# The gate values of a hybrid trunk as one product of 512 columns per layer, and their normalisation in one chain

## The chip, the cores and the metric

The kernel runs on one core of one Trainium2 chip. The metric is the device time of one execution in microseconds, the median of several runs. A core has a matmul engine (TensorE, PE in the profile) with its own loading of weights (PEld), VectorE (DVE), ScalarE (ACT), GpSimd (POOL) and SyncE (SP), which here issues the loads. Each engine works through its own queue in order; semaphores tie the queues together.

## The reference

Two layers over 512 tokens of 1024 numbers, all float32. Each layer has a mixing block (a gating MLP beside differential attention) and a convolutional feed-forward block.

```python
D_SGU, SGU_GROUPS, CHUNK = 512, 4, 128      # gate values: 4 groups of 128 columns
...
n = rmsnorm(h, attn_norm[l])
proj = n @ w_in[l]
u, v_sgu, q, k, v_att = jnp.split(proj, [...], axis=-1)
v_sgu = jax.nn.gelu(v_sgu)
vg = rmsnorm(v.reshape(B, S, SGU_GROUPS, SGU_GROUP_DIM), v_gain)      # per token and group
mixed = jnp.einsum('gpq,bcqgd->bcpgd', w, vg) + b_s.T[None, None, :, :, None]   # w: lower triangle of w_s
y_sgu = u * mixed
...
q = apply_partial_rope(q, cos, sin); k = apply_partial_rope(k, cos, sin)
scores = einsum('bqhmd,bkhmd->bhmqk', qb, kb) * scale     # softmax, difference of two maps, times v
```

The change touches only how `v_sgu` (the gate values) is computed and normalised.

## The kernel before

**Arithmetic.** A float32 product is made from three fast products of numbers split into a high and a low part: high by high, high by low, low by high. A split is a cast (the high part, names that end in h) and a subtraction (the low part, names in l). Weights come in blocks of 128x1024 (`raw`), which ScalarE casts to `wh`, and GpSimd (in halves of 512) or VectorE subtracts to `wl`. Names carry the number of the block: `wh8` is block 8; layer 1's blocks begin at 96, so block 104 is to layer 1 what block 8 is to layer 0. Loads run two blocks ahead of the products (`AHEAD`).

**Input products.** The 128x512 activations `gh_a`, `gl_a` (one of 8 per contraction step k) meet the weights in stages: gate values (`vs`), q, k, attention values (`va`), u. Gate values and va have tokens on the partitions (`tok_gemm`: per k and token tile t three products of 256 columns, two token tiles in a bank); q, k and u have features there (`feat_gemm`: products of 512 columns). The gate values of two pairs of groups, gp 0 and 1, are separate stages. In layer 0 the first of them runs with q in one loop (`both_first`), from half tiles of weights that `opening()` loads and splits itself (`or`, `oh`, `ol`); nine idle products stand ahead of it on TensorE. Then in both layers: the other gate half, k of heads 0 and 1, va, and the score phase.

**What sets the order.** The code is written out in the order in which each engine gets it: `pin` (L119) ties every instruction to the one before it on its engine, so nearly all rows carry L119. `products()` is a generator of steps, one per k; after each step `run` pops one piece of work off the list `due` for the other engines. Forty steps run before the scores, then `flush()` empties `due`. In the score phase each unit (head, query tile) takes one more step and one piece off `later`.

**Work on the gate values.** `gate_work(gp, banks)` makes gelu on ScalarE (`vs`), squares (`vq`, ScalarE), sums (VectorE, `gs`), the reciprocal root of 8 columns (`rsqrt`, 12 small VectorE operations), the normalisation (`normed`, VectorE) and the split (`part`, `vg`). `spatial()` masks the weights `wsp` on GpSimd and splits them (`wsh`, `wsl`). `rope` turns q and k: per head a shuffle (`q_0sh`) and a product from the bank (`q_0t`) on VectorE, a product and a sum on GpSimd (for k's first head on VectorE), then a split (`q_0h`, `q_0l`). The scores of unit 0 read `q_0h`, `q_0l`, `k_0h`, `k_0l`.

In layer 0 the second gate half's work beyond gelu lies in `later`:

```python
g = gate_work(1, banks)
due.extend(g[:2])
later.extend([lambda: (spatial(), g[2](), g[3]())] + g[4:])
```

In layer 1 all of it, and `spatial()`, is done before the scores; `later` has only the split of k's second head.

Of the kernel before, what the change touches and what calls it, by code (L numbers as in the profile page):

```python
# [21 lines left out]
P = 128  # L22
# [47 lines left out]
def trunk(ctx: ExitStack, tc, a, out):  # L70
# [72 lines left out]
    for l in range(DEPTH):  # L143
        specs += [a["w_in"][l, c] for c in range(20)]
# [11 lines left out]
    def block(i):  # L156
        while len(loaded) <= min(i + AHEAD[0], len(specs) - 1):
            j = len(loaded)
            n = specs[j].shape[-1]
# [6 lines left out]
            (sync if j < 6 else nc.sync).dma_start(out=raw, in_=specs[j])  # L166
# [10 lines left out]
    def opening():  # L177

        first = [[], []]
        for m in range(KD):  # L180
            sync.dma_start(out=hT[m], in_=a["xT"][m])
            c = slice(m % 2 * 256, m % 2 * 256 + 256)
            if m % 2 == 0:
                tiles = [(fslot(f"or{b}_{m}"), slot(f"oh{b}_{m}"), slot(f"ol{b}_{m}")) for b in range(2)]
            for b, (r, h, lo) in enumerate(tiles):
                spec = specs[2 * b + m // 4]
                sync.dma_start(out=r[:, c], in_=spec[:, m % 4 * 256 : (m % 4 + 1) * 256])
                first[b].append((h[:, c], lo[:, c]))
# [5 lines left out]
            for b, (r, h, lo) in enumerate(tiles):  # L194
# [51 lines left out]
    def tok_step(banks, x, w, first, last):  # L246
        (xh, xl), (h, lo) = x, w
        for t in range(NT):
            ts = slice(t * P, (t + 1) * P)
            o = banks[t // 2][:, t % 2 * 256 : t % 2 * 256 + 256]  # L250
            mm(o, xh[:, ts], h, start=first and t % 2 == 0, stop=False)
            mm(o, xh[:, ts], lo, start=False, stop=False)
            mm(o, xl[:, ts], h, start=False, stop=last and t % 2 == 1)

    def tok_gemm(banks, xs):

        for k, x in enumerate(xs):
# [3 lines left out]
            tok_step(banks, x, (h[:, c], lo[:, c]), k == 0, k == len(xs) - 1)  # L261
            yield

# [188 lines left out]
    for l in range(DEPTH):  # L452
# [101 lines left out]
        vg, us, ya, ys = [None] * 2, [None] * NG, [None] * NH, [None] * NG  # L554

        def gate_work(gp, banks):

            gs = sm.tile([P, 8], F32, tag="gs", name=f"gs{l}_{gp}", bufs=2)
            vts, sqs, vg[gp] = [None] * 2, [None] * 2, [None] * 2
            r = []  # L560

            def gelu(b):
                vts[b] = tmp(f"vs{l}_{gp}_{b}")
                for x in range(2):
                    c = slice(x * 256, x * 256 + 256)
                    t = 2 * b + x
                    act.activation(vts[b][:, c], banks[b][:, c], AF.Gelu_apprx_tanh, scale=norm.rcol[:, t : t + 1])

            def square(b):
                sqs[b] = tmp(f"vq{l}_{gp}_{b}")  # L570
                act.activation(sqs[b], vts[b], AF.Square)

            def sums(b):
                dve.reduce_sum(
                    gs[:, 4 * b : 4 * b + 4], sqs[b].rearrange("p (x d) -> p x d", d=P), axis=mybir.AxisListType.X
                )
# [5 lines left out]
            def normed(b):  # L582
                v3 = vts[b].rearrange("p (x d) -> p x d", d=P)
                rb = r[0][:, 4 * b : 4 * b + 4].unsqueeze(2).to_broadcast([P, 4, P])
                dve.tensor_tensor(out=v3, in0=v3, in1=rb, op=ALU.mult)

            def part(b):
# [598 lines left out]
```

## Time and profile before

| | |
|---|---|
| median of 3 runs | 1136.31 us (1135.13 to 1136.41) |
| profiled execution | 1136.36 us, of which its span is 1134.6 us |
| TensorE busy | 1115.3 us, 98% of the span |
| VectorE, ScalarE, GpSimd busy | 687.8, 478.4, 412.6 us |
| mean granted clock of TensorE | .996 of full |

The span runs from the first to the last instruction that the trace holds; 1.76 us of the execution lie around it. Busy times are sums over the whole span, so a stage can have another limit than the mean. Matmuls overlap in the records: the pitch from start to start is their cost, not the listed length.

### The profile page before, as it was taken

The numbers are of one execution on the slowest core, as the hardware profiler recorded it, in microseconds if no ns is written. First come the engines' busy times: TensorE is split into PE (matmuls) and PEld (weight loads), VectorE is DVE, ScalarE is ACT, GpSimd is POOL, SyncE is SP. The second block draws the span as 40 slices with busy tenths as digits, with TensorE's granted clock in tenths as the row PEclk, the third lists the DMA queues.
The fourth block names the chain that finished last, engine by engine and source line by source line (L and its number), as shares of the span: only waits on it lengthen the run. The fifth ranks groups of instructions, "written<-read, shape, count | busy, mean of one in ns | idle before, by whom it ended". The sixth has DMA issues, their size and how long they took to land.

```text
span 1134.6 us, 14944 instructions
## 1 busy us (share of the span) xinstructions
PE 1115.3 (98%) x5637; PEld 935.4 (82%) x5637; DVE 687.8 (61%) x1271; ACT 478.4 (42%) x810; POOL 412.6 (36%) x390
## 2 busy tenths in 40 slices
PE   9998999999999999999999999999999999999996
PEld 7986888888888888888899788888888888888886
DVE  7778874775662247664357887767657522666634
ACT  6453553544442134443334554454444312444351
POOL 0466333533222103333557642353313310332351
PEclk9999999999999999999999999999999999999998
DMA  8221112332333232223332221122233323222322
GB/s 272 75 82 50 57 65 94 95 104 89 104 93 97 91 110 93 93 84 93 103 120 80 77 73 57 56 92 95 95 109 93 96 92 110 93 93 93 92 76 75
DMA packets 34215, 105.24 MB, mean 93 GB/s; under 512 B 4064, under 2 KB 8544, under 8 KB 34144
## 3 DMA queue, kind: packets, MB, share of 16 engines
q1 hardware_dynamic: 33712, 104.27, 28.7%
q8 instruction: 44, 0.72, 0.3%
q14 instruction: 27, 0.22, 0.1%
q10 hardware_dynamic: 432, 0.03, 0.0%
HBM read 102.19 MB, written 2.10 MB: 92 GB/s over the span
## 4 chain that ended last, share of the span: by engine, by line
PE 85%; DVE 9%; ACT 3%; POOL 2%; issue 1%; DVEq 0%; ACTq 0%; POOLq 0%
PE g L119 21%; PE v L119 21%; PE dn L119 19%; PE wo L119 7%; PE u L119 4%; PE vs L119 3%; PE q L119 3%; PE dl L119 3%; PE sc L119 1%; ACT wh L119 1%; DVE s L119 1%; PE mx L119 1%; PE av L119 1%; POOL wl L119 1%; ACT s L119 1%
## 5 line engine op out<-in xcount | busy, mean ns | idle before, releaser
L119 POOL TENSOR_TENSOR wl<-raw,wh 128x512 fp32r<-128x512 f32 x187 | 255.4, 1387 | 567.2 <-ACT wh L119 556.4
L119 ACT CAST wh<-raw 128x1024 fp32r<-128x1024 f32 (+1 forms) x192 | 194.3, 1015 | 373.2 <-issue 180.3
L119 DVE TENSOR_TENSOR wl<-raw,wh 128x1024 fp32r<-128x1024 f32 (+1 forms) x96 | 121.2, 1263 | 131.7 <-ACT wh L119 131.6
L119 PE MATMUL v<-gh_f,wh 128*128 128x512 f32 x352 | 137.3, 390 | 0.0
L119 PE MATMUL v<-gh_f,wl 128*128 128x512 f32 x352 | 137.0, 389 | 0.0
L119 PE MATMUL v<-gl_f,wh 128*128 128x512 f32 x352 | 137.0, 389 | 0.0
L119 PE MATMUL g<-gh_f,wl 128*128 128x512 f32 x352 | 137.0, 389 | 0.0
L119 PE MATMUL g<-gh_f,wh 128*128 128x512 f32 x352 | 136.9, 389 | 0.0
L119 PE MATMUL g<-gl_f,wh 128*128 128x512 f32 x352 | 136.9, 389 | 0.0
L119 DVE SCALAR_TENSOR_TENSOR cv<-up_cv,par,cv 128x512 f32<-128x512 f32 x88 | 74.0, 885 | 6.4 <-ACT cv L119 6.1
L119 PEld LDWEIGHTS v<-gh_f,wl 128*128 128x128 f32 x352 | 66.1, 188 | 13.8
L119 PEld LDWEIGHTS g<-gl_f,wh 128*128 128x128 f32 x352 | 66.1, 188 | 13.7
L119 PEld LDWEIGHTS g<-gh_f,wl 128*128 128x128 f32 x352 | 66.1, 188 | 13.7
L119 PEld LDWEIGHTS g<-gh_f,wh 128*128 128x128 f32 x352 | 66.1, 188 | 13.7
L119 PEld LDWEIGHTS v<-gl_f,wh 128*128 128x128 f32 x352 | 66.1, 188 | 13.6
L119 PEld LDWEIGHTS v<-gh_f,wh 128*128 128x128 f32 x352 | 66.1, 188 | 13.6
L119 DVE SCALAR_TENSOR_TENSOR cg<-up_cg,par,cg 128x512 f32<-128x512 f32 x88 | 69.6, 841 | 6.0 <-ACT cg L119 5.6
L119 DVE TENSOR_TENSOR up_cv<-v,rstd_f 128x512 f32<-128x512 f32 x44 | 30.2, 692 | 67.3 <-PE v L119 67.2
L119 DVE TENSOR_TENSOR up_cg<-g,rstd_f 128x512 f32<-128x512 f32 x44 | 30.0, 691 | 57.8 <-PE g L119 54.9
L119 ACT ACTIVATE s<-s,mn 128x128 f32<-128x128 f32 (+3 forms) x64 | 35.5, 555 | 60.1 <-DVE mn L119 55.3
L119 DVE TENSOR_TENSOR hT<-dn,hT 128x512 f32<-128x512 f32 x28 | 19.1, 690 | 46.7 <-PE dn L119 46.7
L119 ACT ACTIVATE cg<-cg 128x512 f32<-128x512 f32 x44 | 27.7, 630 | 45.8 <-DVE cg L119 45.8
(604 smaller groups left out, 2611.2 us busy)
## 6 DMA issues: line engine op xcount, KB each, us to landing
raw<-in_w_up SPq DMA_DIRECT2D x88, 512.0 KB, 3.4
raw<-in_w_dn SPq DMA_DIRECT2D x40, 512.0 KB, 3.5
raw<-in_w_in SPq DMA_DIRECT2D x36, 512.0 KB, 3.4
raw<-in_w_out SPq DMA_DIRECT2D x16, 512.0 KB, 3.4
hT<-in_xT SPq DMA_DIRECT2D x8, 256.0 KB, 4.5
or<-in_w_in SPq DMA_DIRECT2D x16, 128.0 KB, 4.2
raw<-in_w_dn SPq DMA_DIRECT2D x8, 256.0 KB, 3.4
out<-y SPq DMA_DIRECT2D x8, 256.0 KB, 2.2
```

The costliest lines, as they stand in the source:

```text
L119: return lambda *args, **kw: pin(getattr(self.engine, op)(*args, **kw))
```

## The change

The weights of the gate values become four wide blocks per layer (two contraction steps by 512 columns, each filled by two transfers), first in the layer's list. `tok_wide` makes per step and token tile three products of 512 columns, each token tile in a bank of its own: banks 0 and 1 are of the kind that scores use, 2 and 3 of the products' kind. Both layers now run gate values, q, k, va in this order. `opening()` loads tiles of 512 columns by two transfers and splits each in one cast and one subtraction. `gate_work` works by token tile, with one sum tile of 16 columns and one root. Of the normalisation and split, token tiles 0 and 1 come before the scores, 2 and 3 in units 1 to 4 of the score phase. `spatial()` stands at the same step in both layers.

```diff
@@ block
-            (sync if j < 6 else nc.sync).dma_start(out=raw, in_=specs[j])
+            queue = sync if j < 6 else nc.sync
+            if wide:
+                for at, half in enumerate(specs[j]):
+                    o = raw.rearrange("p (k i c) -> p i k c", k=2, i=2)[:, at]
+                    queue.dma_start(out=o, in_=half.rearrange("p (k c) -> p k c", k=2))
+            else:
+                queue.dma_start(out=raw, in_=specs[j])
@@ opening
+            r, h, lo = fslot(f"or{m}"), slot(f"oh{m}"), slot(f"ol{m}")
+            for i, half in enumerate(specs[m // 2]):
+                sync.dma_start(out=r[:, i * 256 : i * 256 + 256], in_=half[:, m % 2 * 256 : m % 2 * 256 + 256])
+            first.append((h, lo))
             if m == 0:
-                r, h, lo = tiles[0]
-                dve.tensor_copy(h[:, c], r[:, c])
-                dve.tensor_sub(lo[:, c], r[:, c], h.bitcast(F32)[:, c])
+                dve.tensor_copy(h, r)
+                dve.tensor_sub(lo, r, h.bitcast(F32))
             norm.scaled(m)
-            for b, (r, h, lo) in enumerate(tiles):
-                if m > 0 or b > 0:
-                    act.copy(h[:, c], r[:, c])
-                    dve.tensor_sub(lo[:, c], r[:, c], h.bitcast(F32)[:, c])
+            if m > 0:
+                act.copy(h, r)
+                dve.tensor_sub(lo, r, h.bitcast(F32))
@@ tok_wide (new)
+    def tok_wide(banks, xs, ws=None):
+        for k, x in enumerate(xs):
...
+            for t in (0, 2):
+                tok_step([(t + i, banks[t + i], True, True) for i in range(2)], x, w, k == 0, k == len(xs) - 1)
+                yield
@@ gate_work
+            gs = sm.tile([P, NT * NG], F32, tag="gs", name=f"gs{l}", bufs=1)
...
-                r.append(rsqrt(gs, 8, f"gr{l}_{gp}"))
+                r.append(rsqrt(gs, NT * NG, f"gr{l}"))
@@ products
-            if l == 0:
-                yield from both_first()
-                banks = value_banks(1, sc_bank)
-                yield from tok_gemm(banks, xs)
-                g = gate_work(1, banks)
-                due.extend(g[:2])
-                later.extend([lambda: (spatial(), g[2](), g[3]())] + g[4:])
-            else:
-                yield from gate_values(0)
-                yield from queries(0)
-                yield from gate_values(1)
+            banks = [sc_bank(f"vs{t}_{l}") for t in range(2)] + [mm_bank(f"vs{t}_{l}") for t in (2, 3)]
+            yield from tok_wide(banks, xs, first if l == 0 else None)
+            gelu, sums, root, normed, part = gate_work(banks)
...
+            due.extend(([nothing] * 4 if l == 0 else []) + [of(gelu, 2, 3), of(gelu, 0, 1)])
+            q = query_banks(0)
+            yield from feat_gemm(q, xs)
+            turn0, turn1, part0, part1 = rope(q, qs, 0, "q")
+            due.extend([turn0, turn1, of(sums, 0, 1), of(sums, 2, 3), root, part0, part1])
+            due.extend(of(f, t) for f in (normed, part) for t in range(2))
+
+            later.extend(of(f, t) for f in (normed, part) for t in (2, 3))
@@ steps of a layer
         run(steps, 28 - (22 if l == 0 else 15))
-        if l > 0:
-            spatial()
+        spatial()
         run(steps, 12)
```

The queue of GpSimd in layer 0, from block 7's low part on, before (the last number of a name is a tile's own):

```order
L119 TENSOR_TENSOR wl7_571<-raw7_569,wh7_570 128x512 x2
L119 TENSOR_TENSOR q0_0sh_634<-q0_0sh_634,sr0_619 128x512
L119 TENSOR_TENSOR q0_0t1_636<-q0_0t1_636,q0_0sh_634 128x512
L119 TENSOR_TENSOR q0_1sh_652<-q0_1sh_652,sr0_619 128x512
L119 TENSOR_TENSOR q0_1t1_654<-q0_1t1_654,q0_1sh_652 128x512
L119 TENSOR_TENSOR wl8_663<-raw8_661,wh8_662 128x512 x2
L119 TENSOR_TENSOR wl9_718<-raw9_716,wh9_717 128x512 x2
L119 TENSOR_TENSOR wl10_761<-raw10_759,wh10_760 128x512 x2
```

and after:

```order
L119 TENSOR_TENSOR wl7_483<-raw7_481,wh7_482 128x512 x2
L119 TENSOR_TENSOR wl8_540<-raw8_538,wh8_539 128x512 x2
L119 TENSOR_TENSOR q0_0sh_551<-q0_0sh_551,sr0_521 128x512
L119 TENSOR_TENSOR q0_0t1_553<-q0_0t1_553,q0_0sh_551 128x512
L119 TENSOR_TENSOR q0_1sh_563<-q0_1sh_563,sr0_521 128x512
L119 TENSOR_TENSOR q0_1t1_565<-q0_1t1_565,q0_1sh_563 128x512
L119 AFFINE_SELECT wsp0_281<-wsp0_281 128x512
L119 TENSOR_TENSOR wsl0_284<-wsp0_281,wsh0_283 128x512
L119 TENSOR_TENSOR wl9_598<-raw9_596,wh9_597 128x512 x2
```

Block 8's low part moved ahead of q's rope, and the spatial weights (`wsp`, `wsl`), which stood far behind, moved between the rope and block 9.

The queue of VectorE in layer 0, around the first root, before; the first piece ends with the root's first operation, the second begins with its last:

```order
L119 STREAM_SHUFFLE q0_1sh_652<-q1_0_308 128x512
L119 TENSOR_TENSOR q0_1t1_654<-q1_0_308,cr0_611 128x512
L119 TENSOR_REDUCE gs0_0_505<-vq0_0_0_674 128x4
L119 TENSOR_REDUCE gs0_0_505<-vq0_0_1_682 128x4
L119 TENSOR_TENSOR q0_0l_713<-q0_0t1_636,q0_0h_712 128x512
L579 TENSOR_SCALAR gs0_0_505<-gs0_0_505 128x8
```

and, still before, the second piece:

```order
L389 SCALAR_TENSOR_TENSOR gr0_0_693<-gr0_0t_694,gr0_0_693 128x8
L119 TENSOR_TENSOR q0_1l_730<-q0_1t1_654,q0_1h_729 128x512
L119 TENSOR_TENSOR vs0_0_0_588<-vs0_0_0_588,gr0_0_693 128x512
L119 TENSOR_TENSOR vs0_0_1_603<-vs0_0_1_603,gr0_0_693 128x512
L119 TENSOR_TENSOR vg0_0_0l_754<-vs0_0_0_588,vg0_0_0h_753 128x512
L119 TENSOR_TENSOR vg0_0_1l_779<-vs0_0_1_603,vg0_0_1h_778 128x512
L119 STREAM_SHUFFLE k0_0sh_824<-k0_0_659 128x512
```

and the same two places after:

```order
L119 STREAM_SHUFFLE q0_1sh_563<-q1_0_443 128x512
L119 TENSOR_TENSOR q0_1t1_565<-q1_0_443,cr0_513 128x512
L119 TENSOR_REDUCE gs0_441<-vq0_0_575 128x4
L119 TENSOR_REDUCE gs0_441<-vq0_1_578 128x4
L119 TENSOR_REDUCE gs0_441<-vq0_2_587 128x4
L119 TENSOR_REDUCE gs0_441<-vq0_3_590 128x4
L594 TENSOR_SCALAR gs0_441<-gs0_441 128x16
```

and its second piece:

```order
L409 SCALAR_TENSOR_TENSOR gr0_610<-gr0t_611,gr0_610 128x16
L119 TENSOR_TENSOR q0_0l_630<-q0_0t1_553,q0_0h_629 128x512
L119 TENSOR_TENSOR q0_1l_640<-q0_1t1_565,q0_1h_639 128x512
L119 TENSOR_TENSOR vs0_0_504<-vs0_0_504,gr0_610 128x512
L119 TENSOR_TENSOR vs0_1_506<-vs0_1_506,gr0_610 128x512
L119 TENSOR_TENSOR vg0_0l_685<-vs0_0_504,vg0_0h_684 128x512
L119 TENSOR_TENSOR vg0_1l_701<-vs0_1_506,vg0_1h_700 128x512
L119 STREAM_SHUFFLE k0_0sh_716<-k0_0_536 128x512
```

There are four sums instead of two ahead of the root, and the root's columns are 16 instead of 8. The low part of q's first head moved from ahead of the root to behind it; from there to k's shuffle the rest stands as before.

## Rows read from the trace of the kernel before

**Rows 1.** Part 1 of the page: busy us, share of span, instructions

```profile
PE 1115.3 (98%) x5637; PEld 935.4 (82%) x5637; DVE 687.8 (61%) x1271; ACT 478.4 (42%) x810; POOL 412.6 (36%) x390
```

**Rows 2.** Timeline of TensorE, layer 1: start, length, instruction, wait before it

```profile
566.11 0.28 PE L119 MATMUL vs<-wh,gh_a 128*128 128x256 f32 x1
...
577.62 0.40 PE L119 MATMUL q<-gh_a,wh 128*128 128x512 f32 x1
...
601.01 0.40 PE L119 MATMUL k<-gh_a,wh 128*128 128x512 f32 x1
...
611.92 0.28 PE L119 MATMUL va<-wh,gh_a 128*128 128x256 f32 x1
...
624.13 0.33 PE L119 MATMUL sc<-k_0l,q_0h 64*128 64x128 f32 x2 [0.29 <-DVE k_0l L119]
...
624.50 0.50 PE L119 MATMUL q<-gh_a,wh 128*128 128x512 f32 x1
```

**Rows 3.** Timeline of TensorE, layer 0, and the first wo of layer 1

```profile
41.88 0.40 PE L119 MATMUL k<-gh_a,wh 128*128 128x512 f32 x1
...
64.87 0.50 PE L119 MATMUL q<-gh_a,wh 128*128 128x512 f32 x1
...
157.88 0.45 PE L119 MATMUL wo<-yah,wh 128*128 128x512 f32 x1
...
713.37 0.44 PE L119 MATMUL wo<-yah,wh 128*128 128x512 f32 x1
```

**Rows 4.** Timeline of TensorE, the opening of layer 0

```profile
1.28 4.02 PE L119 MATMUL idle<-zeros 128*128 128x512 bf16 x9 [1.28 <-DVE zeros L136]
...
4.74 0.77 PE L119 MATMUL vs<-oh,gh_a 128*128 128x256 f32 x1
...
6.83 0.37 PE L119 MATMUL vs<-ol,gh_a 128*128 128x256 f32 x1
7.04 0.28 PE L119 MATMUL vs<-oh,gl_a 128*128 128x256 f32 x1
...
8.90 0.28 PE L119 MATMUL vs<-oh,gh_a 128*128 128x256 f32 x1
```

**Rows 5.** Timeline of ScalarE, the opening: the second half tile

```profile
5.62 0.40 ACT L119 CAST oh<-or 128x256 fp32r<-128x256 f32 x1 [0.98 <-DMA or<-in_w_in]
```

**Rows 6.** Timeline of VectorE, layer 0: the first root (L384 to L389 by rsqrt)

```profile
46.65 1.25 DVE L579 TENSOR_SCALAR gs<-gs 128x8 f32<-128x8 f32 x1
...
51.69 0.17 DVE L388 TENSOR_TENSOR gr_0t<-gr_0t,gr 128x8 f32<-128x8 f32 x1
```

**Rows 7.** Timeline of GpSimd, layer 0, around the same root

```profile
40.88 1.29 POOL L119 TENSOR_TENSOR q_0sh<-q_0sh,sr 128x512 f32<-128x512 f32 x1 [2.14 <-DVE q_0sh L119]
...
46.13 5.49 POOL L119 TENSOR_TENSOR wl<-raw,wh 128x512 fp32r<-128x512 f32 x4
```

**Rows 8.** Timeline of VectorE, layer 1, gate sums to k_0l

```profile
607.33 1.28 DVE L119 TENSOR_REDUCE gs<-vq 128x4 f32<-128x512 f32 x2 [1.82 <-ACT vq L119]
...
614.94 1.29 DVE L119 TENSOR_TENSOR vs<-vs,gr 128x512 f32<-128x512 f32 x2
...
617.54 0.75 DVE L119 STREAM_SHUFFLE k_0sh<-k 128x512 f32<-128x512 f32 x1
...
622.62 1.45 DVE L119 TENSOR_TENSOR k_0l<-k_0t,k_0h 128x512 fp32r<-128x512 f32 x1
```

**Rows 9.** Timeline of GpSimd, layer 1, the spatial weights

```profile
609.13 0.63 POOL L119 TENSOR_SCALAR_AFFINE_SELECT wsp<-wsp 128x512 f32<-128x512 f32 x1
...
610.49 1.30 POOL L119 TENSOR_TENSOR wsl<-wsp,wsh 128x512 fp32r<-128x512 f32 x1 [0.73 <-ACT wsh L119]
```

**Rows 10.** Timeline of ScalarE, layer 1, the cast of a block of weights

```profile
604.27 1.05 ACT L119 CAST wh<-raw 128x1024 fp32r<-128x1024 f32 x1
```

**Rows 11.** Windows at the end: start:end, length, busy us by engine, granted clock, DMA

```profile
1124.00:1126.00 2.00, 0.41 (x2) 0.20 (x2) 1.34 (x4) 0.51 (x1) 0.00 (x0) 1.00 0.95 332
1126.00:1128.00 2.00, 0.40 (x2) 0.40 (x3) 1.31 (x7) 0.20 (x1) 0.00 (x0) 0.65 0.00 0
```

More of the change, by code (lines that the diff above doesn't have):

```diff
@@ L143, in trunk @@
     for l in range(DEPTH):
-        specs += [a["w_in"][l, c] for c in range(20)]
+        w = a["w_in"][l]
+        specs += [[w[c + k // 4][:, k % 4 * 256 : k % 4 * 256 + 512] for c in (0, 4)] for k in range(0, KD, 2)]
+        specs += [w[c] for c in [2, 3] + list(range(6, 20))]
         specs += [a["w_out"][l, c] for c in range(8)]
@@ L158, in block @@
             j = len(loaded)
-            n = specs[j].shape[-1]
+            wide = isinstance(specs[j], list)
+            n = 1024 if wide else specs[j].shape[-1]
             if j >= len(specs) - 6:
@@ L244, in feat_gemm, with tok_step @@
             yield
-    def tok_step(banks, x, w, first, last):
+    def tok_step(outs, x, w, first, last):
         (xh, xl), (h, lo) = x, w
-        for t in range(NT):
+        for t, o, opens, closes in outs:
             ts = slice(t * P, (t + 1) * P)
-            o = banks[t // 2][:, t % 2 * 256 : t % 2 * 256 + 256]
-            mm(o, xh[:, ts], h, start=first and t % 2 == 0, stop=False)
+            mm(o, xh[:, ts], h, start=first and opens, stop=False)
             mm(o, xh[:, ts], lo, start=False, stop=False)
-            mm(o, xl[:, ts], h, start=False, stop=last and t % 2 == 1)
+            mm(o, xl[:, ts], h, start=False, stop=last and closes)
     def tok_gemm(banks, xs):
+        outs = [(t, banks[t // 2][:, t % 2 * 256 : t % 2 * 256 + 256], t % 2 == 0, t % 2 == 1) for t in range(NT)]
         for k, x in enumerate(xs):
@@ L552, in values, with gate_work, gelu, sums @@
             ])
[L554 to L559, printed above, removed]
+        vg, us, ya, ys = [None] * NT, [None] * NG, [None] * NH, [None] * NG
+        def gate_work(banks):
+            gs = sm.tile([P, NT * NG], F32, tag="gs", name=f"gs{l}", bufs=1)
+            vts, sqs = [None] * NT, [None] * NT
             r = []
[L562 to L573, printed above, removed]
+            def gelu(t):
+                vts[t] = tmp(f"vs{l}_{t}")
+                act.activation(vts[t], banks[t], AF.Gelu_apprx_tanh, scale=norm.rcol[:, t : t + 1])
+            def sums(t):
+                sqs[t] = tmp(f"vq{l}_{t}")
+                act.activation(sqs[t], vts[t], AF.Square)
                 dve.reduce_sum(
-                    gs[:, 4 * b : 4 * b + 4], sqs[b].rearrange("p (x d) -> p x d", d=P), axis=mybir.AxisListType.X
+                    gs[:, NG * t : NG * t + NG], sqs[t].rearrange("p (g d) -> p g d", d=P), axis=mybir.AxisListType.X
                 )
@@ L622, in mix @@
                 osl = bm[:, t * P : (t + 1) * P]
-                vh, vl = vg[g // 2][t // 2]
-                o = (t % 2 * 2 + g % 2) * P
-                vsl = slice(o, o + P)
+                vh, vl = vg[t]
+                vsl = slice(g * P, g * P + P)
                 mm(osl, vh[:, vsl], ws_h[:, g, :], start=True, stop=False)
```

54 lines of the change are left out of this document (17 added, 37 removed).

## The prediction

> **What bounds the kernel now.** I read the page's busy times first: TensorE works 1115.3 of the span's 1134.6 us [rows 1], so an edit can gain by shortening TensorE's own work and loses wherever TensorE has to wait. Next, TensorE's timeline of layer 1's input products [rows 2]: gate values 0 take 566.11 to 577.62, k starts at 601.01, va at 611.92. In these stretches nothing waits. A gate half is 96 products of 256 columns in 11.51 us, .1199 each; k is 48 products of 512 columns in 10.91 us, .2273 each. The first break comes at the scores: the second score product starts at 624.13 after waiting .29 for k_0l, and the scores end at 624.50. So k's chain on VectorE and GpSimd already ends last here, by a little. In layer 0 the scores end at 64.87, 22.99 after k's start at 41.88 [rows 3]. The score phases, from the end of these scores to the first wo, do the same products in both layers, yet take 93.01 us in layer 0 (64.87 to 157.88) and 88.87 in layer 1 (624.50 to 713.37) [rows 2, 3].
>
> **TensorE's own work.** The change replaces 192 products of 256 columns per layer by 96 of 512: 192 x .1199 - 96 x .2273 = 23.0 - 21.8, about 1.2 us per layer, **-2.4**. The Trainium skill ("TensorE: Matmul & The Clock Gate", section on 56 against 53.3 ns) has another figure: a fixed cost of about 2.5 ns per product at the full clock. The two pitches of the rows give 2 x .1199 - .2273 = 12.5 ns per product instead. By the page the saving would be an estimated .5 us over both layers and the time 1.9 us later; the rows are this kernel's, so I keep -2.4.
>
> **The opening of layer 0.** Now the first product starts at 4.74, from a half tile of 256 columns [rows 4]; the next half lands at 5.62 [rows 5]. After the change one cast of 512 columns needs both halves. A cast of 256 took .40 on ScalarE there; I take .6 for 512 on VectorE, so the first product starts at 6.2. Its low part (a subtraction of 512 columns, .65 by half of the pair at 614.94 [rows 8]) allows the second at 6.85, and the low part of the activations, now behind it on VectorE, the third near 7.5. Nine products remain of k=0: 9 x .23 ends it near 9.7 at the full clock. Before, k=0 ended at 8.90, and the same pair of levels shows there: a product that starts at 6.83 is followed .21 later, from 7.04 on the records are as short as in layer 1. The clock rose 5.7 us after TensorE began at 1.28 with its nine idle products, without a break. Now there are breaks from 5.3 to 7.5, so the rise may come later. Both bounds: +.8 if it still rises at 7.0, and +2.2 if all nine products run at the lower level (.43 each). I take the late one, nearest to what the row shows (the rise followed unbroken work). k then starts at 41.88 - 1.2 + 2.2 = 42.9 (41.5 with the early rise).
>
> **The transfers.** The wide blocks come by two transfers each instead of one. Blocks are loaded two ahead (AHEAD), and at 566.11 and 601.01 TensorE goes over to the next product without a wait for weights [rows 2], so I take 0. Were that cover gone, the nearest such wait is the opening's .98 [rows 5].
>
> **The chain to the scores.** This decides. Call k's start S. What follows is a schedule in order of the queues, made with durations from rows.
> - ScalarE's cast of wh8 takes 1.05 [rows 10] and waits for a tile that q frees at S. GpSimd's wl8 now stands before the rope of q, not behind it; two such operations take 2.7 (5.49 for four [rows 7]): it ends at S+3.7. This is 104 in place of 8 in layer 1.
> - The rope's four operations took 40.88 to 46.13, 5.25 [rows 7]: the first head is done at S+6.3, the second at S+8.9. The selection wsp (.63) follows to S+9.5; wsl starts .73 later and takes 1.30, to S+11.6 [rows 9]. Then wl9 and wl10, 1.3 for each half.
> - ScalarE's fourth square needs the tile that q_0t's sum frees at S+6.3; with a reduction of .64 (half of 1.28 [rows 8]) the root can begin at S+7.6.
> - The root is 12 small operations on VectorE, now 12 for all four token tiles instead of twice 12. Free, one takes .17 (51.69). But at 46.65 the first one lasted 1.25, and the others lasted as long until GpSimd's wl of 46.13 ended at 51.62 [rows 6, 7]: each operation on SBUF that starts beside a GpSimd operation ends with it. So operations 1 and 2 end at S+8.9 and S+9.5 (rope and wsp), 3 to 6 fit into GpSimd's pause, 7 ends with wsl at S+11.6, 8 to 11 with the halves of wl9 and wl10 at S+16.8, the twelfth at S+17.0. Half of the operations on the chain is thus dear, as in layer 0 before.
> - Behind the root on VectorE, before k's first shuffle, stand q_0l, q_1l, two normed and two vg low parts: 6 x .65 (1.29 for two [rows 8]) = 3.9, to S+20.9.
> - From k's shuffle (617.54) to the end of k_0l (622.62 + 1.45) were 6.53 us [rows 8], and the scores ended .43 after it [rows 2]: they end at S+27.8.
>
> Without any wait it would be S+23.0, as layer 0 shows. Layer 1: S = 601.01 - 1.2 = 599.8, scores end at 627.6 instead of 624.50, **+3.1**. Layer 0: 42.9 + 27.8 = 70.7 instead of 64.87, **+5.8** (both contain the saving and the opening). The waiting of TensorE is some 4.8 us per layer, in two pieces, for k_0h and then for k_0l, with little work between.
>
> **The score phases.** Before, layer 0's units 1 to 8 carried the second gate half's squares, sums, root and the spatial weights; this leaves them. Its phase should come down to layer 1's, 93.01 - 88.87 = 4.14. What remains in both layers are two normed and two parts more in units 1 to 4 than layer 1 had; I take .3 for them (bounds 0, hidden under the products of a unit, and 2.6, four operations of .65 all exposed): **-3.8** and **+.3**.
>
> **The clock.** At the end of the kernel TensorE had .41 us of work from 1124 to 1126 at the full clock, .40 in the next two with a mean clock of .65 [rows 11]: with only the two levels that is full speed until about 1126.6 and half of it after. So it falls to 1.2 GHz some 2.6 us after work thins out. A wait of 4.8 us with a few small products in it comes up to this. If it falls, TensorE runs at half speed until it rises; in the opening that took 5.7 us, so half of that, 2.9, is lost at most, and 0 at least. I take 1.4 per layer, **+2.8**.
>
> **Sum.** 3.1 + .3 + 5.8 - 3.8 + 2.8 = +8.2 on the profiled execution's own 1136.36 us, 1144.6. That execution lies .05 above the median of the runs: **1144.5**.
>
> **Rivals.** A measurement of this kernel can tell about .2%, 2.3 us, from no change.
> - *The chain is late, the clock stays.* For it: the waits come in two pieces with products between. Sum +5.4, with the early rise +4.0: 1139 to 1142. Chance .18.
> - *Partly late.* If GpSimd's and VectorE's operations interleave better (the root starting before the rope ends, or finding wl9 late because its DMA or cast is late), some of the 4.8 us goes: 1134 to 1139. Chance .18.
> - *Faster: the chain fits.* The place is k_0l in both layers: it must end 4.8 us sooner, at S+22.6. The point from which this decides is how many of the root's operations are held: with all 12 at .2 the chain is 5 to 6 us shorter. For it: the root's operations that meet no GpSimd operation run at .2 (51.69), and every late block of weights would give it such a pause. Against: in the queue only wsl's .73 is a pause by construction, and behind it stand four halves of wl. Then layer 1 gives -1.2 - .3 (the wait at 624.13) + .3 and layer 0 -1.2 + 2.2 - 3.8 (1.4 less with the early rise): together -4.0 to -5.4, 1131 to 1132. Chance .15.
> - *The saving fails,* as the Trainium skill's fixed cost per product, above, would have it: 1.9 us more in whichever case. Against it stand two pitches in this trace; 1 in 20, within the ranges.
>
> **Numbers.** The forecast (chain late, clock falls) has .49, with 1141.5 to 1148 as its own range (each clock term 0 to 2.9, the opening's 1.4). Faster .15, no change .18, slower .49 + .18 = .67. The range from 1134.5 to 1148 leaves out the fitting case and little else.
>
> **What would show it.** In the changed kernel's trace: k's start near 41.5 to 42.9 and 599.8; the root's operations at 1.2 us beside wl9 and wl10; the first scores of unit 0 waiting for VectorE's k_0l or ScalarE's k_0h some 4 us after va's end; a granted clock below 1 in that window; layer 0's score phase near 89 us; 512-column products at .227. Wrong it would be if the root runs at .2 each and the scores follow va without a break.

## The result: 1145.03 us, slower by 0.8%

The changed kernel takes 1145.03 us (median of 4 runs, 1143.93 to 1145.74) against 1136.28 for the kernel before: a ratio of 1.0080, with a 95% interval of 1.0068 to 1.0093. Its profiled execution took 1145.74 us with a span of 1143.8, 9.2 more than before.

Part 1 of its page (columns as in [rows 1]) shows TensorE with 192 instructions less and yet 2.9 us more busy time, which is a first sign of a lower clock (the windows below show it):

```profile
PE 1118.2 (98%) x5445; PEld 928.5 (81%) x5445; DVE 684.6 (60%) x1239; ACT 476.7 (42%) x794; POOL 411.2 (36%) x390
```

TensorE's timeline of layer 0, at the places of [rows 3] (start, length, instruction, wait before it):

```profile
43.04 0.39 PE L119 MATMUL k<-gh_a,wh 128*128 128x512 f32 x1
...
68.16 0.33 PE L119 MATMUL sc<-k_0h,q_0h 64*128 64x128 f32 x2 [2.57 <-ACT k_0h L119]
70.06 0.47 PE L119 MATMUL sc<-k_0l,q_0h 64*128 64x128 f32 x2 [1.57 <-DVE k_0l L119]
...
70.67 0.79 PE L119 MATMUL q<-gh_a,wh 128*128 128x512 f32 x1
...
162.24 0.44 PE L119 MATMUL wo<-yah,wh 128*128 128x512 f32 x1
```

Two waits are new: 2.57 us for ScalarE's k_0h, then 1.57 for VectorE's k_0l. k starts at 43.04 instead of 41.88, the scores end at 70.67 instead of 64.87. Layer 1, at the places of [rows 2]:

```profile
570.44 0.39 PE L119 MATMUL vs<-wh,gh_a 128*128 128x512 f32 x1
...
604.02 0.39 PE L119 MATMUL k<-gh_a,wh 128*128 128x512 f32 x1
...
629.21 0.33 PE L119 MATMUL sc<-k_0h,q_0h 64*128 64x128 f32 x2 [2.64 <-ACT k_0h L119]
631.11 0.33 PE L119 MATMUL sc<-k_0l,q_0h 64*128 64x128 f32 x2 [1.57 <-DVE k_0l L119]
...
631.47 0.57 PE L119 MATMUL q<-gh_a,wh 128*128 128x512 f32 x1
...
722.50 0.44 PE L119 MATMUL wo<-yah,wh 128*128 128x512 f32 x1
```

From the first gate product to k it is 33.58 us, where it was 34.90; from k to the end of the scores 27.45, where it was 23.49. Granted clock in windows of layer 0 (columns as in [rows 11]; the clock is the third number from the end):

```profile
66.00:68.00 2.00, 0.00 (x0) 0.00 (x0) 2.00 (x3) 0.51 (x1) 0.91 (x1) 1.00 0.08 8
68.00:70.00 2.00, 0.33 (x2) 0.19 (x2) 2.00 (x4) 1.39 (x2) 1.73 (x2) 0.64 0.67 252
70.00:72.00 2.00, 1.94 (x7) 1.64 (x8) 1.70 (x4) 0.36 (x2) 1.13 (x1) 0.50 0.01 2
...
74.00:76.00 2.00, 2.00 (x8) 1.59 (x7) 1.93 (x6) 1.56 (x5) 1.42 (x2) 0.65 0.00 0
76.00:78.00 2.00, 2.00 (x13) 1.36 (x12) 1.38 (x4) 0.00 (x0) 0.00 (x0) 1.00 0.66 205
```

TensorE does next to nothing from 65.6 to 70.1. Only the two levels 1.00 and .50 occur here, so the means put the fall at about 68.6 (.64 from 68 to 70) and the return at about 75.4 (.65 from 74 to 76): TensorE's clock is at the lower level, 1.2 GHz, for 6.8 us. In layer 1 the same windows from 630 read .94, .50 and .71, which is the lower level from about 631.8 to 635.2.

The loss in terms of time, from the marks of both traces (the score phase runs from the end of unit 0's scores to the first wo): layer 0's scores end 5.80 later; its score phase is 91.57, 1.44 shorter; the feed-forward blocks are the same (408.20 and 408.23 from wo to the next gate product). Layer 1 wins 1.32 ahead of k, loses 3.96 from k to the scores, and 2.16 in its score phase (91.03 against 88.87). 5.80 - 1.44 - 1.32 + 3.96 + 2.16 = 9.16 of the span's 9.2.

VectorE around layer 0's root, and then from the last low part to k_0l (answers to [rows 6] and [rows 8]):

```profile
50.78 1.23 DVE L594 TENSOR_SCALAR gs<-gs 128x16 f32<-128x16 f32 x1
52.04 0.55 DVE L404 TENSOR_SCALAR gr<-gs 128x16 int32<-128x16 int32 x1
52.62 0.17 DVE L405 TENSOR_SCALAR gs<-gs 128x16 f32<-128x16 f32 x1
...
53.47 1.17 DVE L407 TENSOR_TENSOR gr0t<-gs,gr 128x16 f32<-128x16 f32 x1
...
58.43 1.22 DVE L408 TENSOR_TENSOR gr0t<-gr0t,gr 128x16 f32<-128x16 f32 x1
59.67 0.18 DVE L409 SCALAR_TENSOR_TENSOR gr<-gr0t,gr 128x16 f32<-128x16 f32 x1
...
63.57 0.75 DVE L119 STREAM_SHUFFLE k_0sh<-k 128x512 f32<-128x512 f32 x1
...
68.60 1.40 DVE L119 TENSOR_TENSOR k_0l<-k_0t,k_0h 128x512 fp32r<-128x512 f32 x1
```

GpSimd beside it (answers to [rows 7] and [rows 9]), and ScalarE's fourth square (the last line):

```profile
44.19 2.56 POOL L119 TENSOR_TENSOR wl<-raw,wh 128x512 fp32r<-128x512 f32 x2 [4.28 <-ACT wh L119]
...
50.70 1.28 POOL L119 TENSOR_TENSOR q_1t<-q_1t,q_1sh 128x512 f32<-128x512 f32 x1
51.93 0.63 POOL L119 TENSOR_SCALAR_AFFINE_SELECT wsp<-wsp 128x512 f32<-128x512 f32 x1
53.30 1.31 POOL L119 TENSOR_TENSOR wsl<-wsp,wsh 128x512 fp32r<-128x512 f32 x1 [0.73 <-ACT wsh L119]
54.56 5.05 POOL L119 TENSOR_TENSOR wl<-raw,wh 128x512 fp32r<-128x512 f32 x4
...
49.39 0.63 ACT L119 ACTIVATE vq<-vs 128x512 f32<-128x512 f32 x1 [3.02 <-POOL q_0t L119]
```

Put side by side: the root's first operation ends at 52.01 with q_1t (51.98), the second at 52.59 with wsp (52.56), four run at .17 in GpSimd's pause of .73, the seventh ends at 54.64 with wsl, the eighth to eleventh take 1.22 each and end with the halves of wl9 and wl10, and the twelfth, after 59.61, takes .18. The root itself can't begin sooner, because the fourth square stands 3.02 us until the rope's q_0t sets its tile free.

The opening, at the places of [rows 4]:

```profile
6.04 0.77 PE L119 MATMUL vs<-oh,gh_a 128*128 128x512 f32 x1 [0.74 <-DVE oh L119]
...
7.34 0.80 PE L119 MATMUL vs<-oh,gl_a 128*128 128x512 f32 x1
...
10.07 0.61 PE L119 MATMUL vs<-oh,gl_a 128*128 128x512 f32 x1
10.49 0.42 PE L119 MATMUL vs<-oh,gh_a 128*128 128x512 f32 x1
...
11.21 0.40 PE L119 MATMUL vs<-oh,gh_a 128*128 128x512 f32 x1
```

The first product starts 1.30 later than before; the pitch is .43 from 7.93 on, and .23 only from about 10.5. The granted clock is listed as 1.00 from the start of every trace here, also where the pitch is .43; so in the opening the lower level is read from the pitch alone, and the column does not confirm it.

### The profile page after: what moved, and what is told of

It reads as the page before. It is cut to its first block, busy times and chain, and to the rows that moved or that the text cites. A ratio compares the mean times of both kernels' runs of the same rounds, so it can differ in the third digit from the quotient of the medians.

```text
span 1143.8 us, 14548 instructions
## 1 busy us (share of the span) xinstructions
PE 1118.2 (98%) x5445; PEld 928.5 (81%) x5445; DVE 684.6 (60%) x1239; ACT 476.7 (42%) x794; POOL 411.2 (36%) x390
## 4 chain that ended last, share of the span: by engine, by line
PE 85%; DVE 8%; POOL 3%; ACT 2%; issue 2%; DMA 0%; SPq 0%; DVEq 0%; POOLq 0%; ACTq 0%
PE g L119 21%; PE v L119 20%; PE dn L119 19%; PE wo L119 7%; PE vs L119 4%; PE u L119 4%; PE q L119 4%; PE dl L119 3%; POOL wl L119 1%; PE sc L119 1%; PE mx L119 1%; DVE s L119 1%; PE av L119 1%; ACT s L119 1%; ACT wh L119 1%
```

## The experiments

Each was compared with the kernel before on the same chip. S is the start of k's first product. The marks come from one profiled execution of each kernel, which lies up to 1.6 us from the kernel's median, and further in one case that is named.

**Sums and root ahead of q's rope** (e1_root_first).

```diff
-            due.extend(... + [of(gelu, 2, 3), of(gelu, 0, 1)])
+            due.extend(... + [of(gelu, 2, 3), of(gelu, 0, 1), of(sums, 0, 1), of(sums, 2, 3), root])
...
-            due.extend([turn0, turn1, of(sums, 0, 1), of(sums, 2, 3), root, part0, part1])
+            due.extend([turn0, turn1, part0, part1])
```

> The gate values' sums and root are put ahead of q's rope, into the steps of q, and the normalisation behind q's split; nothing else changes. If the changed kernel loses because its root runs beside GpSimd's work behind the rope (held 1.2 us per operation) and so delays k_0l, the root here runs before GpSimd's wl8, at about .2 each, in layer 1 wholly before k starts; the scores follow va with less than 1 us of waiting, the granted clock stays full there, and the time falls by some 4 us of waiting and 2.3 us of half clock per layer, to 1131 to 1134 us. Rival, that VectorE simply has too much work between q and the scores, wherever the root stands: the scores stay as late as 27 us after k's start and the time stays above 1141 us.

Measured: 1138.80 us, ratio 1.0028 (1.0017 to 1.0039), 3.0 us above the kernel before instead of 8.75, with an edit of the order alone. Layer 1 did as expected: the only wait left is .90 for k_0l, the scores end at S+24.07, and the clock stays full:

```profile
626.45 0.33 PE L119 MATMUL sc<-k_0l,q_0h 64*128 64x128 f32 x2 [0.90 <-DVE k_0l L119]
...
626.82 0.50 PE L119 MATMUL q<-gh_a,wh 128*128 128x512 f32 x1
```

In layer 0 sums and root came too late to be ahead of anything (the squares wait on ScalarE, and the root's operations mixed with the rope), the waits are still 1.09 and 1.57, the scores end at S+26.15, and the clock falls. The time is above the range expected, since layer 0 kept most of its loss and layer 1's score phase is 90.35.

**The root in PSUM** (e2_root_psum). The root's sums and its scratch column lie in a PSUM bank; y stays in SBUF.

```diff
-            gs = sm.tile([P, NT * NG], F32, tag="gs", name=f"gs{l}", bufs=1)
+            inb = []
...
+                    inb.append(tr_bank(f"gs{l}"))
+                gs = inb[0][:, : NT * NG]
...
+                gs, t = inb[0][:, :n], inb[0][:, n : 2 * n]
...
-                r.append(rsqrt(gs, NT * NG, f"gr{l}"))
+                r.append(rsqrt(gs, n, f"gr{l}", t))
```

> The root stays where the change put it, but its sums and its scratch column lie in a PSUM bank, so that each of its operations reads at most one operand from SBUF. If two SBUF operands beside a GpSimd operation are what holds an operation, the root's twelve take .2 each, some 2.6 us instead of 9; q's and the gate's low parts, behind it, then meet wl9 and wl10 instead and are held in its place, so k's first shuffle comes only about 2.7 us sooner. The wait before the scores falls from 4.2 to about 1.5 us, the clock stays full: 1134 to 1137 us (1139 to 1141 if the clock falls all the same). Rival, that the operations last 1.2 us for another reason (a wait of their own, the issue): they stay at 1.2 and the time stays within 1 us of 1145.

Measured: 1144.09 us, ratio 1.0077 (1.0061 to 1.0092): a miss: 8.3 above the kernel before where 8.75 stood, a difference within the intervals, and some 8 to 11 were expected. The mechanism was right and its worth was not. VectorE of layer 0:

```profile
50.63 0.18 DVE L600 TENSOR_SCALAR gs<-gs 128x16 f32<-128x16 f32 x1
...
52.22 0.17 DVE L410 SCALAR_TENSOR_TENSOR gr<-gs,gr 128x16 f32<-128x16 f32 x1
54.63 1.61 DVE L119 TENSOR_TENSOR q_0l<-q_0t,q_0h 128x512 fp32r<-128x512 f32 x1 [2.23 <-ACT q_0h L119]
56.17 0.17 DVE L408 TENSOR_TENSOR gs<-gs,gr 128x16 f32<-128x16 f32 x1
56.25 1.69 DVE L119 TENSOR_TENSOR q_1l<-q_1t,q_1h 128x512 fp32r<-128x512 f32 x1
...
58.28 1.36 DVE L119 TENSOR_TENSOR vs<-vs,gr 128x512 f32<-128x512 f32 x1
```

and GpSimd beside it:

```profile
53.14 1.30 POOL L119 TENSOR_TENSOR wsl<-wsp,wsh 128x512 fp32r<-128x512 f32 x1 [0.74 <-ACT wsh L119]
54.39 4.70 POOL L119 TENSOR_TENSOR wl<-raw,wh 128x512 fp32r<-128x512 f32 x3
```

The root's operations take .17 beside the same GpSimd work: so it was the SBUF operands that held them. But the low parts behind them are now held instead (q_0l 1.61, q_1l 1.69, normed 1.36). q_0l waits for ScalarE's cast anyway, and in this kernel's order the root's last three operations stand behind it. GpSimd pays too: three halves of wl take 4.70 where they took 3.80. k's shuffle comes only .8 sooner. What is late is the whole of both engines' work behind S, with ScalarE's cast in it, not the root by itself.

**Blocks 8 to 10 on VectorE** (e6_relief). The low parts of blocks 8, 9 and 10 of both layers.

```diff
-            eng = gps if (j > 6 and i_l != 27 if i_l < 28 else j % 3 == 1) else dve
+            eng = gps if (j > 6 and i_l not in (8, 9, 10, 27) if i_l < 28 else j % 3 == 1) else dve
```

> Order as in the changed kernel, but the low parts of blocks 8, 9 and 10 of each layer are VectorE's (1.26 us for a whole block) instead of GpSimd's (2.5). If the two engines' shared time is the bound, GpSimd is through with the rope and the spatial weights 2.5 us sooner and then leaves VectorE alone: most of the root's operations run at .2, k's first shuffle comes 2 to 4 us sooner, and the time falls to 1134 to 1140 us. Rival, that VectorE's own load is the bound: with 3.8 us more on it the scores come later still, 1147 us or more.

Measured: 1143.40 us (1139.83 to 1144.03), ratio 1.0061 (1.0047 to 1.0074). The root's operations ran at .17 but for the first, though the last sum still waited for the rope, and the scores end at S+25.96 and S+26.11: 1.3 to 1.7 sooner, less than expected. Both waits stay, 1.14 and 1.57 in layer 0. The median is neither theory's time. The profiled execution is the fastest of the four, 3.6 us below the median; its early k (41.27) may be a part of that. That VectorE's load took back part of what GpSimd's gave fits, but was not shown apart.

**Normalisation behind k's rope** (e7_behind_k).

```diff
-            due.extend(of(f, t) for f in (normed, part) for t in range(2))
+            gate = [of(f, t) for f in (normed, part) for t in range(2)]
...
             yield from keys(0)
+            due.extend(gate)
             yield from values(0)
```

> Order as in the changed kernel, but normalisation and split of token tiles 0 and 1 stand behind the rope of k's first heads instead of ahead of it: four operations of .65 less before k's first shuffle. The scores come 2.6 us sooner in each layer; the second wait, 1.57 for k_0l behind k_0h, stays, and with it most likely the fall of the clock. What was moved then delays unit 0's softmax by up to 2.6. Chain as bound: 1138 to 1142 us. Rival, that the place behind the scores costs as much as it gives: within 1 us of 1145.

Measured: 1143.84 us, ratio 1.0072 (1.0058 to 1.0086). The scores are on time (S+23.60 and S+23.70): 4.0 and 3.8 us sooner where 2.6 were expected, and the second wait, which was to stay, came down to .42 and .52. But what was moved is paid for behind them, and the total lies between the two ranges, nearer to the rival's: the score phases are 94.49 and 94.52, since unit 1's scores now wait for VectorE's first pass over unit 0, and the clock falls behind that wait (.91 and .50 in the windows from 70):

```profile
71.30 0.69 PE L119 MATMUL sc<-k_0h,q_0h 64*128 64x256 f32 x2 [2.38 <-DVE mn L119]
```

**The chain in q's steps** (e5_in_q; with eleven idle products).

```diff
-            due.extend(([nothing] * 4 if l == 0 else []) + [of(gelu, 2, 3), of(gelu, 0, 1)])
+            due.extend([of(gelu, 2, 3), of(gelu, 0, 1), of(sums, 0, 1), of(sums, 2, 3)])
+            due.extend([root, of(normed, 0, 1), of(part, 0), of(part, 1)])
...
-            due.extend([turn0, turn1, of(sums, 0, 1), of(sums, 2, 3), root, part0, part1])
-            due.extend(of(f, t) for f in (normed, part) for t in range(2))
+            due.extend([turn0, turn1, part0, part1])
```

> The gate chain of token tiles 0 and 1 as a whole (gelu, sums, root, normalisation, split) stands in the eight steps of q, ahead of q's rope, without the four empty steps of layer 0; eleven idle products at the start. If what delays the scores is the number of VectorE operations on SBUF that fall into GpSimd's unbroken stretch behind k's start, only q's two low parts are left in it: k_0l is ready when va ends, neither layer waits more than .5 us for it, the clock stays full, and the time is 1130 to 1133 us, below the kernel before. Rival, that the wide products or the score phases keep the loss: 1136 us or more with the scores on time.

Measured: 1139.29 us, ratio 1.0031 (1.0019 to 1.0043). Layer 1 is the case expected: the scores end at S+23.64 and wait for nothing, va waits .42, and the clock stays full. What it still lacks against before is its score phase, 90.39 instead of 88.87: the normalisation of token tiles 2 and 3, left for units 1 and 2, goes with a late unit 3, where the transposes of the softmax weights wait for an earlier unit's `aTl`, the low part of those weights (e8_best below, which leaves none of this work for the units, has .48 there):

```profile
650.59 0.44 PE L119 MATMUL at<-ident,s 128*128 128x128 f32 x2 [1.45 <-DVE aTl L119]
```

Layer 0 failed in its own way: the chain stood ahead of the tables' products on VectorE (cr at 46.90), q's rope began at 50.57, and va waited 1.76 for block 9's low part. TensorE also stood 2.21 us at 40.69, ahead of the tables' transposes, for which the profile names no cause.

**The clock in the waits** (e4_fill and e9_fill2). Idle bfloat16 products keep TensorE busy ahead of unit 0's first scores, in the second kernel also between those with k_0h and those with k_0l.

```diff
+        fill = sc_bank(f"fill{l}")
+        for i in range(11):
+            mm(fill, zeros[:, :P], zeros, start=True, stop=True)
...
+                    if st and self is units[0]:     # e9_fill2 alone
+                        more = tr_bank(f"more{l}")
+                        for i in range(8):
+                            mm(more, zeros[:, :P], zeros, start=True, stop=True)
```

> Eleven idle bfloat16 products of 512 columns (.215 each, 2.4 us) stand on TensorE between the last va product and the first score of each layer, where it waits for k_0h; the chain to k_0l is untouched. If the waiting drops TensorE to 1.2 GHz and that costs 2.3 us per layer, the granted clock stays full after the scores and the time falls by 4 to 4.6 us, to about 1140.5; the scores themselves come no sooner. Rival, that the half clock costs nothing because the score phase waits for other engines anyway: the clock stays full and the time falls by less than 1 us.

Measured: 1143.32 us, ratio 1.0068 (1.0056 to 1.0081). The fall came all the same, only later (the second wait, 1.56, stayed), so this run says nothing on the price of half clock.

> The changed kernel with TensorE kept busy in both waits of unit 0 of each layer: eleven idle products ahead of the first scores and eight (1.7 us) between the products with k_0h and those with k_0l. The scores come no sooner. If the half clock costs what the pitch shows (ten products of q at .43 instead of .23), q's second stage runs at .23 from the start and each score phase is 1.5 to 2.2 us shorter: 1140.5 to 1142 us, with an opening like the changed kernel's. Rival, that the clock falls for another reason than TensorE's waiting: it falls all the same and the time stays within 1 us of 1144.

Measured: 1142.78 us, ratio 1.0058 (1.0043 to 1.0073). That is a little above the range expected. Now the clock holds; its windows in layer 0:

```profile
68.00:70.00 2.00, 2.00 (x12) 0.88 (x10) 2.00 (x3) 0.87 (x1) 1.92 (x2) 1.00 0.54 190
70.00:72.00 2.00, 2.00 (x12) 1.62 (x11) 1.66 (x8) 0.89 (x2) 0.60 (x1) 1.00 0.03 8
```

The score phases are 89.81 and 89.93 instead of 91.57 and 91.03: the half clock cost 1.8 and 1.1 by these two traces, and without it layer 0's phase is 3.2 shorter than before. Two other kernels with the same score phase and a fall of the clock, e4_fill and e3_idle11 below, have 90.92 and 90.94 in layer 0 and 91.01 and 90.80 in layer 1, so 1.1 to 1.8 and .9 to 1.1 is what the traces bear. In the medians filling both waits is worth 2.1 us (6.7 above the kernel before instead of 8.75).

**Eleven idle products** (e3_idle11: `range(9)` becomes `range(11)` in the opening).

> Two more idle products at the start, eleven instead of nine, nothing else. If the clock rises later than before because TensorE pauses between the idle products and the first gate products, here the pause before the first product (6.04) is filled, the pitch turns to .23 near 7 to 8 us instead of 10.5, and the time falls by 0.8 to 1.6 us. Rival, that the rise has nothing to do with the pause: the pitch still turns at 10.5 and the time is the same within .3 us, or .1 later.

Measured: 1143.74 us, ratio 1.0075 (1.0062 to 1.0087). In the profile the pitch is .23 from 7.75 on and k starts at 41.59, 1.45 sooner. But the edit did not do what it was made for: the first product still waited .80 us, since the eleven idle products ended at 5.31, where nine had ended at 5.30. The pitch had thus turned before they were over, after the same unbroken work in which it had not turned with nine. With nine idle products and the same opening the break before the first product was .74, .86, 1.03, .81 and .76 us in five kernels, and k started at 43.04, 42.65, 42.88, 42.70 and 42.50; in two more (blocks on VectorE, normalisation behind k) it was .50 and .23, and k started at 41.27 and 40.97. In these seven the two early starts go with the two short breaks; here an early start came with a break of .80. So what sets the moment stays open, and the timed difference is within what the openings vary by.

**Towards a faster version** (e8_best, e10_split). In e8_best layer 1's chain of all four token tiles stands in q's steps; layer 0 has sums and root ahead of q's rope. The root's operations are tied together in the queue, and eleven idle products stand at the start, in both kernels.

```diff
+            chain = [of(gelu, 2, 3), of(gelu, 0, 1), of(sums, 0, 1), of(sums, 2, 3), root]
+            if l == 0:
+                chain[2:2] = [nothing] * 3
+            else:
+                chain += [of(normed, 0, 1, 2, 3), of(part, 0, 1), of(part, 2, 3)]
+            due.extend(chain)
...
```

> In layer 1 the whole gate chain, all four token tiles, stands in q's eight steps and nothing of it is left for the score phase. In layer 0 gelu comes at once, sums and root as the last thing ahead of q's rope (the root's operations kept together), the rest as in the changed kernel. Eleven idle products at the start. If the lost time is the chain, in the scores' wait and in what was left for the score phase: layer 1 takes 33.6 us from its first gate product to k, 23 to 23.7 from k to the end of the first scores and 89 to 89.4 to the first wo, 1 us less than before; layer 0's scores end 23 to 25 us after k starts, without a fall of the clock; the time is 1131 to 1135 us. Rival, that the chain only moves its wait elsewhere (to va, to k's weights): 1138 us or more.

Measured: 1141.74 us, ratio 1.0048 (1.0036 to 1.0061); the rival was right. Layer 1's score phase is 88.73, as before the change, so what was left for the units was the whole of that loss (90.39 in the kernel with the chain in q). But the longer chain pushes q's rope, and with it block 9's low part behind it on GpSimd, beyond va's need, in both layers:

```profile
620.94 0.58 PE L119 MATMUL va<-wl,gh_a 128*128 128x256 f32 x1 [1.77 <-POOL wl L119]
```

The clock falls behind this wait as well (.73 and .50 in the windows from 620). e10_split keeps tiles 2 and 3 for units 1, 4, 5 and 6 and gives layer 0's block 9 to VectorE:

```diff
+                chain += [of(normed, 0, 1), of(part, 0), of(part, 1)]
...
+            later.extend([of(normed, 2), nothing, nothing, of(normed, 3), of(part, 2), of(part, 3)])
...
+            eng = gps if (j > 6 and j != 9 and i_l != 27 if i_l < 28 else j % 3 == 1) else dve
```

> The best halves together. Layer 1: the chain of token tiles 0 and 1 in q's steps, as the kernel with the chain in q had it (scores 23.6 after k's start, clock full). Layer 0: gelu, sums and root ahead of q's rope, and block 9's low part (attention values' second block) on VectorE, since GpSimd brought it too late there. In both layers the pieces left for the score phase stand in units 1, 4, 5 and 6 instead of 1 to 4, where they delayed unit 3 by 1.4. Eleven idle products at the start. If these three places (the scores' wait, va's weights, unit 3) are all that stood against the saving of 1.3 per layer: layer 0's scores 23 to 24 after k's start, phases of 89 to 90, the clock full throughout, 1131.5 to 1134.5 us. Rival, that a new place turns late: above 1136 us.

Measured: 1138.85 us, ratio 1.0031 (1.0021 to 1.0041). Layer 1: 33.60, 23.66 and 90.19, together 147.45, as long as before (147.26); other units for the pieces cost as much as units 1 to 4 did. Layer 0's scores end at S+27.37: its chain did not fit.

**Layer 1 alone** (e11_layer1, e12_split_ws). Layer 0 is the kernel before's. Layer 1 has the wide product, the whole chain in q's steps, both blocks of va split by VectorE, and the spatial weights in unit 1.

```diff
...
+            due.extend([of(gelu, 2, 3), of(gelu, 0, 1), of(sums, 2, 3), of(sums, 0, 1), root])
+            due.extend([of(normed, 0, 1, 2, 3), of(part, 0, 1), of(part, 2, 3)])
+            later.append(spatial)
...
```

> Layer 0 exactly as in the kernel before (gate halves, q beside the first, half tiles in the opening). Layer 1 alone with the wide product; its gate chain of all four token tiles in q's steps, the low parts of the attention values' two blocks on VectorE, the spatial weights in the score phase (unit 1). If the wide product is worth what TensorE's pitch says and only its chain costs, layer 1 goes from its first gate product to the first wo in 145.4 to 146.4 us, against 147.26 before, with its score phase near 88.8, and the time is .9 to 1.8 below the kernel before: ratio .998 to .9995. Rival, that wherever the chain is put it costs the saving again (va's weights or k_0l late by a microsecond, with or without the clock): 147 us or more, ratio 1.000 or above.

Measured: 1136.19 us, ratio 1.0007 (.9998 to 1.0016). Ahead of the scores the saving is there: 33.60 and 23.79, 1.00 less than before. But the score phase is 92.03. ScalarE's queue in unit 1:

```profile
635.64 0.62 ACT L119 CAST wsh<-wsp 128x512 fp32r<-128x512 f32 x1 [3.07 <-POOL wsp L119]
636.17 0.61 ACT L119 ACTIVATE s<-s,mn 128x384 f32<-128x384 f32 x1
```

and TensorE's in unit 3:

```profile
647.92 0.44 PE L119 MATMUL at<-ident,s 128*128 128x128 f32 x2 [2.19 <-DVE aTl L119]
```

ScalarE stands 3.07 us before wsh, since GpSimd's mask is queued behind a block's low part; unit 2's exponentials stand behind it. The clock falls behind the wait of 2.19 too (.79 and .50 in the two windows from 648). Layer 0, whose code is the kernel before's, has the same wait at the same place. In the kernel before:

```profile
89.77 0.66 PE L119 MATMUL at<-ident,s 128*128 128x128 f32 x4 [1.87 <-DVE aTl L119]
...
90.00:92.00 2.00, 2.00 (x14) 1.75 (x13) 2.00 (x4) 0.29 (x1) 1.63 (x1) 1.00 0.00 0
```

and in this one:

```profile
89.05 0.85 PE L119 MATMUL at<-ident,s 128*128 128x128 f32 x4 [1.83 <-DVE aTl L119]
...
90.00:92.00 2.00, 2.00 (x6) 1.52 (x6) 2.00 (x8) 0.35 (x2) 2.00 (x2) 0.50 0.00 0
```

The same wait was followed by the full clock in one execution and by half of it in the other, so the length of a wait does not decide this by itself. Nor did the half clock lengthen that phase (92.92 against 93.01): unit 7's wait shrank from 1.75 to .55. The last kernel parts mask and split in both layers; in layer 1:

```diff
-                later.append(spatial)
+                later.extend([mask_ws] + [nothing] * 3 + [split_ws])
```

> As the kernel with the wide product in layer 1 alone, but the masking of the spatial weights (GpSimd, unit 1) and their split (ScalarE's cast and GpSimd's subtraction, unit 5) stand apart in both layers. In the trace of that kernel, and of the kernel before in layer 0, ScalarE waited over 3 us in unit 1 for GpSimd's mask, with unit 2's exponentials queued behind it, and TensorE waited some 2 us in unit 3. If that wait is what ate the saving of layer 1, its score phase falls from 92.0 to 89 us, without a fall of the clock, and layer 0's by 1.5 to 1.9 (93.0 to 91.2): 1131.5 to 1133.5 us, ratio .996 to .998. Rival, that unit 3 is late for another reason (the rope of q's third head behind a block's low part): both stay, and the ratio is 1.000 or above.

Measured: 1135.87 us, ratio 1.0002 (.9993 to 1.0011). The cause was right: unit 3's wait is .53 in layer 1 and .38 in layer 0. But the time is not the one expected. The split, now in unit 5, stands on GpSimd between the two ropes of k and makes unit 7 late, in layer 0 later than it was (1.75 at 110.25 in the kernel before):

```profile
109.55 0.44 PE L119 MATMUL at<-ident,s 128*128 128x128 f32 x2 [3.13 <-DVE aTl L119]
```

In layer 1 the same wait is 1.23 at 667.21, where the kernel before has none above .3 us. The clock falls behind layer 0's wait (.68 and .50 from 110 to 114). The phases are 94.15 and 90.23. The profiled executions of these two kernels took 1137.44 and 1137.48 us against medians of 1136.19 and 1135.87, so the usual execution loses less than these phases say. No version tried beats the kernel before.

## Why the prediction was right, point by point

- *TensorE's own work.* Right: 34.90 became 33.58, 1.32 per layer where 1.2 was forecast. The fixed cost per product in the Trainium skill ("TensorE: Matmul & The Clock Gate", on 56 against 53.3 ns) would have given an estimated .24 per layer; the trace differs.
- *The opening.* Right in size in this trace, k at 43.04 (42.9), but in part by luck. With the third product at 7.5 and nine more at .43, the late bound comes to 7.5 + 3.9 - 8.9 = +2.5 and not +2.2; six of the nine ran at .43 and three at .23, and k=0 ended at 11.21, +2.3. The reason given, a rise of the clock that waits for unbroken work, is not shown: with eleven idle products the pitch turned before the break, after the work in which it had not turned with nine.
- *The transfers.* Right at 0: no product of the gate values after the first waits.
- *The chain to the scores.* Right: S+27.63 and S+27.45 (27.8), and in layer 0 operation by operation for the root. In layer 0 before, four of the root's twelve operations were held (46.65 to 51.66) and not half, as the prediction says; its schedule for the changed kernel does not rest on that. Of the cause one thing was told too simply: half of the root's operations are dear, but making them cheap gives next to nothing (1144.09), because the next operations are held in their place. The runs fit a bound by the sum of what the engines do on SBUF behind S. What helped was taking work out of it: sums and root ahead of q's rope (1138.80), or the whole chain in q's steps (1139.29). Two parts of the chain were not tested by themselves: the fourth square's wait for the rope, 3.02 us, and the place of the spatial weights between the rope and block 9, 2.7 us of GpSimd (51.93 to 54.61).
- *The score phases.* Mis-sized: -3.8 and +.3 were forecast. With the clock held they were -3.2 (93.01 to 89.81) and +1.1 (88.87 to 89.93). The two normed and two parts left for units cost 1.1 to 1.7 us per layer, not .3 (89.93 against 88.87, and 90.39 with them against 88.73 without, all at full clock), within the bounds of 0 and 2.6.
- *The clock.* Forecast 1.4 per layer; by filling the waits 1.1 to 1.8 in layer 0 and .9 to 1.1 in layer 1. The bound of 2.9 held, but its reason did not: the lower level was to last 5.7 us at most and lasted 6.8 in layer 0, during 1.5 of which TensorE stood anyway.
- *Sum.* +8.2 forecast, +9.4 in the profiled executions, +8.75 in the medians. Errors cancel in it: layer 1's scores came .5 less late than forecast (+2.64 against +3.1), the phases and the clock together cost 1.4 more (+.7 against -.7). The range of 1134.5 to 1148 is wide enough for two of the rivals as well, so the marks within the trace bear the account and not the total.
- *Rivals.* "The chain fits" came true in layer 1 once the chain stood in q's steps (1139.29), and even then the saving of 1.3 went into the score phase, which that rival had priced at .3.

That a VectorE operation with SBUF operands waits for GpSimd's is what the Trainium skill ("SBUF — State Buffer", section "Who interferes with whom") calls an exclusive lock on a shared pair of ports; the kernel with the root in PSUM agrees, .17 against 1.22. The page also counts tensor_scalar, with its one SBUF input, among the operations that can take that pair. The rows agree: L594 is one and took 1.23 beside q_1t, and L405, another, took .17 in GpSimd's pause but 1.21 (at 601.14 of layer 1) in the kernel with the chain in q.

## What to carry to other kernels

Fusing two products saves their overhead at once (1.3 us per layer here) and merges the two chains behind them into one that can't start before both are done. Count the operations of that chain between its start and the first reader, and price each VectorE operation with SBUF operands at a whole GpSimd operation wherever GpSimd's queue is unbroken: here 1.2 us instead of .17. Making such an operation cheap helped little where its neighbours took over the waiting; moving work to a stage in which GpSimd or VectorE is idle did help.

A wait of a nearly always busy TensorE costs its length, and half clock can follow. Behind the waits of unit 0 it did, for .9 to 1.8 us per layer; behind waits of 1.87 and 1.75 us in the kernel before it did not.

## What was not expected of the hardware

Both engines pay: with the root in PSUM, GpSimd's three halves of wl took 4.70 us where they had taken 3.80, while VectorE's long operations ran in between.

One and the same wait, 1.87 and 1.83 us in the same code of layer 0, was followed by the full clock in one kernel's trace and by half of it in another's.

And the moment at which the pitch turns in the opening lay between 6.83 and 10.49 in seven kernels whose openings are the same, which moves k's start between 40.97 and 43.04. That is large enough to account for the changed kernel's spread of 1.8 us, which was not tested.
